# Attention of a hybrid diffusion step: running maxima, biases on ScalarE, weight sums from a column of ones

## The chip, the cores and the metric

The kernel runs on one core of one Trainium2 chip. That core has five engines, each of which runs its own list of instructions in order: TensorE (PE in the profile; its weight loads are shown as PEld), VectorE (DVE), ScalarE (ACT), GpSimd (POOL) and SyncE (SP), which here issues all DMAs. The metric is device time in microseconds (us) of one execution.

## The reference

Two layers are applied to 256 prompt tokens and 2048 latent tokens. Each layer projects the tokens once, runs four mixers beside each other (latent attention, a long convolution called Hyena, a diagonal state space S5, and gated linear attention GLA), gates them and projects back. The change touches the attention alone, which has four heads of query width 96 and value width 64. A latent query reads 512 cached, then 2048 latent keys; a prompt query reads the 256 prompt keys:

```
s  = einsum('bqhd,bkhd->bhqk', q, k) * 96 ** -0.5
pr = softmax(s, axis=-1)
o  = einsum('bhqk,bkhd->bqhd', pr, v)
```

## The kernel before, in words

A unit of attention is one head and one tile of 128 queries. There are 16 latent tiles and 2 prompt tiles, 4 heads and 2 layers, so 128 units with 2560 keys and 16 units with 256. The 2560 keys are cut into three chunks, `CHUNKS = [(0, 1024), (1024, 1024), (2048, 512)]`; a prompt unit has one chunk. Values that must be exact to more than 16 bits are held as a high and a low fp16 part, so a product takes two or three matmuls.

`scores` (line 469) makes one chunk of scores: for each 512 keys three matmuls into one tile `sp` in PSUM (L482 to L484) and a maximum on VectorE (L485); the two maxima of a 1024-key chunk are joined on VectorE (L489) and turned into the bias of the exponential, also on VectorE (L490); ScalarE takes the exponential into `e` and adds up each row into `su` (L492). Each such exponential is followed in the trace by a second ScalarE instruction that reads the sum out (ACTIVATION_READ_ACCUMULATOR). Every chunk has its own maximum.

`values` (line 496) rounds `e` to fp16 on ScalarE or, every third time, on VectorE (L505, L507), takes the remainder on GpSimd (L508), transposes both parts by a DMA (L510, `ph` to `pt`) and multiplies them with the values: per 128 keys one matmul with the high part of the weights against 128 columns (high and low part of `V`), and one with the low part against 64 columns (L514, L515). The three chunks of a unit go to three column blocks of one PSUM tile `om`, of which there is a single buffer.

`combine` (line 517) brings the three chunks to a common maximum: minimum of the biases (L525), factors `al` (L526, ScalarE), the sums times the factors (L527), their total (L528), its reciprocal (L529), the factors times that (L530), and then the three blocks of `om` times their factors, added up (L533, L535), and the high and low columns added (L537). Apart from L526 all of it is on VectorE.

Two chunks are in flight: the loop in `attention` emits the scores of the next chunk before `values` and `combine` of the last one. Heads 0 and 1 come first (stream `side`), heads 2 and 3 later (stream `fill`). Keys and values of a head are loaded by `load` (line 455) into pools of two buffers.

The order of each engine's instructions is not the order of the code: a scheduler plays the whole program through on a model of the machine and, by the priority of each stream, decides which ready instruction of an engine comes next. Hyena, GLA, the filters of the next layer and the output projection run in the same stretches, so what attention takes on an engine also sets where their instructions stand.

Of the kernel before, what the change touches and what calls it, by code (L numbers as in the profile page):

```python
# [8 lines left out]
F32 = mybir.dt.float32  # L9
# [294 lines left out]
def mla_prep(s, l, p, tp, pp):  # L304
# [67 lines left out]
    for t in range(22):  # L372
# [39 lines left out]
        nc.scalar.activation(vd[:, :, 0:64], kv[:, :, 64:128], AF.Copy, scale=sv)  # L412
        nc.vector.scalar_tensor_tensor(out=vd[:, :, 64:128], in0=kv[:, :, 64:128], scalar=sv, in1=vd[:, :, 0:64],
# [38 lines left out]
def attention(s, l, units, tp, kp, bank, ps_o, emit):  # L452
# [17 lines left out]
    def scores(u, c, k0, n):  # L470

        KT = u["KT"]
        e = tp.tile([128, 1024], F32, tag="e", name="e", bufs=3)[:, 0:n]
        nb, su, m = u["nb"], u["su"], u["m"]
        parts = range(0, n, 512)
        sps = []
        for i, a in enumerate(parts):
# [12 lines left out]
        nc.vector.tensor_scalar(out=nb[:, c:c + 1], in0=mc, scalar1=nssc, scalar2=LN2_15, op0=ALU.mult, op1=ALU.add)  # L490
        for i, d in enumerate(sps):
            nc.scalar.activation(e[:, i * 512:min(i * 512 + 512, n)], d, AF.Exp, bias=nb[:, c:c + 1], scale=ssc,  # L492
                                 accum_out=su[:, 2 * c + i:2 * c + i + 1])
        u["e"][c] = e

    def values(u, c, k0, n, first):

        e, V = u["e"].pop(c), u["V"]
        if first:
            u["om"] = ps_o.tile([128, 3, 128], F32, tag="om", name="om")  # L500
# [11 lines left out]
        for i in range(nk):  # L512
            v = V[:, k0 // 128 + i]
            nc.tensor.matmul(om[:, c], lhsT=pt[:, i], rhs=v, start=i == 0, stop=False)  # L514
            nc.tensor.matmul(om[:, c, 0:64], lhsT=pt[:, nk + i], rhs=v[:, 0:64], start=False, stop=i == nk - 1)  # L515

    def combine(u, C):
        nb, su, om = u["nb"], u["su"], u["om"]
        al, dn, mx = small(4, "al"), small(1, "dn"), small(1, "mx")
        w = tp.tile([128, 128], F32, tag="wo", name="wo")  # L520
        sc = su.rearrange("p (c i) -> p c i", i=2)
        last = C - 1
# [31 lines left out]
    for h, t in units:  # L554
        if h not in kv:
            kv[h] = load(h)
        if (h // 2, t) not in pairs:
# [6 lines left out]
        u = dict(h=h, t=t, qt=pairs[h // 2, t][0][:, h % 2], KT=KT, V=V, e={}, m=small(8, "m"), nb=small(4, "nb"), su=small(8, "su"),  # L564
                 ns=5 if t < 16 else 1)
        if C > 1:
            nc.vector.memset(u["su"][:, 5:6], 0.0)
# [1251 lines left out]

PADF = 640  # L1820


def body(tc, I, O, depth=DEPTH):
# [21 lines left out]
    with ExitStack() as top:  # L1845
# [5 lines left out]
        for l in range(depth):  # L1851
# [73 lines left out]
            kp = att.enter_context(pool(name=f"kv{l}", bufs=2, side="right"))  # L1925
            ps_s = att.enter_context(pool(name=f"pss{l}", bufs=3, space=PSUM))
# [89 lines left out]
```

## Time and profile before

| | |
|---|---|
| time, median of 3 runs | 4542.72 us (4534.35 to 4557.65) |
| profiled execution: time, span in the trace | 4533.57 us, 4531.5 us |
| busy in the span: PE, PEld, DVE, ACT, POOL | 3680.5, 2131.0, 3249.0, 2180.7, 2048.0 us |
| the same as shares | 81%, 47%, 72%, 48%, 45% |
| first and last score matmul of attention | 1138.5 us, 4424.4 us |

No engine is busy all the time, and the work of the stages differs: projections fill 0 to about 1133 us and 2455 to 3400 us, attention with its neighbours 1133 to 2455 us (layer 0) and 3400 to 4455 us (layer 1). In the rows further down, `L489` is line 489 of the kernel above, `out<-in` names the tiles of an instruction, and `x256` says how many instructions a row stands for. "Idle before" is the time that the engine waited just before the instructions of a row, and the arrow names what ended the wait.

### The profile page before, as it was taken

To read this page: it belongs to the slowest core of one execution; us is meant where nothing else is said; L and a number is where in the kernel's file an instruction comes from. 1 tells how busy PE (TensorE), PEld (TensorE's weight loads), DVE (VectorE), ACT (ScalarE), POOL (GpSimd) and SP (SyncE) were. 2 spreads that over 40 slices of the span, in tenths; PEclk is the share of its full clock that TensorE was granted. 3 is DMA by queue.
4 is the path that set the end of the run, shared out by engine and by line. 5 is a ranking of instruction groups with operands and counts; after the bars stand their busy time and mean duration, and the time that the engine had idled before them with its cause. 6 is when DMAs were issued, how large, how long until landed. Compare 5 with 4: busy or idle time off the path is not lost.

```text
span 4531.5 us, 67262 instructions
## 1 busy us (share of the span) xinstructions
PE 3680.5 (81%) x21798; PEld 2131.0 (47%) x21798; DVE 3249.0 (72%) x8338; ACT 2180.7 (48%) x4337; POOL 2048.0 (45%) x2052
## 2 busy tenths in 40 slices
PE   6788988778777878778876788889898888667898
PEld 2544544324455555334433644544455555434444
DVE  4765477886788888778774568875447878667884
ACT  3533234546554555675453333363336545646562
POOL 2443343650565655555443234424225545434552
PEclk8999999889888988899998899999998868877999
DMA  6744745656977789896987555633447856999895
GB/s 210 182 120 139 213 122 147 195 136 189 219 184 171 168 203 209 231 243 178 238 204 198 139 132 142 154 105 122 134 147 187 189 135 147 217 233 247 192 187 148
DMA packets 1343432, 799.93 MB, mean 177 GB/s; under 512 B 989588, under 2 KB 1221296, under 8 KB 1341544
## 3 DMA queue, kind: packets, MB, share of 16 engines
q1 hardware_dynamic: 1343080, 795.63, 69.8%
q8 instruction: 173, 2.83, 0.3%
q14 instruction: 179, 1.47, 0.1%
HBM read 352.12 MB, written 207.37 MB: 123 GB/s over the span
## 4 chain that ended last, share of the span: by engine, by line
PE 18%; DVE 16%; DMA 7%; issue 5%; ACT 4%; POOL 2%; SPq 2%; POOLq 0%; DVEq 0%; ACTq 0%
DMA pt<-ph 3%; DVE m L485 2%; PE lv L1603 2%; PE mm L266 2%; PE mm L267 2%; PE mm L268 2%; ACT e L492 2%; DVE m L489 1%; PE mm L1801 1%; PE mm L1802 1%; PE mm L1803 1%; PE sp L482 1%; DVE X L1189 1%; PE om L514 1%; PE sp L484 1%
## 5 line engine op out<-in xcount | busy, mean ns | idle before, releaser
L508 POOL TENSOR_TENSOR ph<-e,ph 128x1024 f16<-128x1024 f32 (+2 forms) x400 | 728.5, 1829 | 636.2 <-ACT ph L505 274.3
L492 ACT ACTIVATE e<-sp,nb,ssc 128x512 f32<-128x512 f32 (+1 forms) x656 | 499.9, 768 | 416.7 <-DVE nb L490 331.6
L266 PE MATMUL mm<-hT,ws 128*128 128x512 f16 (+1 forms) x1440 | 533.0, 370 | 55.1 <-ACT zc L1708 22.5
L485 DVE TENSOR_REDUCE m<-sp 128x1 f32<-128x512 f32 (+1 forms) x656 | 438.6, 676 | 132.6 <-PE sp L484 130.4
L267 PE MATMUL mm<-hT,ws 128*128 128x512 f16 (+1 forms) x1440 | 533.0, 370 | 0.0
L268 PE MATMUL mm<-hT,ws 128*128 128x512 f16 (+1 forms) x1440 | 531.7, 369 | 0.0
L514 PE MATMUL om<-V,pt 128*128 128x128 f16 x2560 | 299.4, 234 | 107.2 <-DMA pt<-ph 60.5
L482 PE MATMUL sp<-KT,qt 128*128 128x512 f16 x640 | 273.0, 427 | 131.3 <-ACT e L492 128.4
L514 PEld LDWEIGHTS <-pt 128*128 128x128 f16 x2592 | 256.2, 108 | 152.7 <-DMA pt<-ph 89.4
L505 ACT CAST ph<-e 128x1024 f16<-128x1024 f32 (+2 forms) x268 | 269.2, 1005 | 88.0 <-DMA pt<-ph 85.8
L515 PE MATMUL om<-V,pt 128*128 128x64 f16 x2560 | 289.7, 205 | 0.0
L515 PEld LDWEIGHTS <-pt 128*128 128x128 f16 x2592 | 245.7, 104 | 62.6 <-issue 48.9
L483 PE MATMUL sp<-KT,qt 128*128 128x512 f16 x640 | 272.6, 426 | 0.0
L484 PE MATMUL sp<-KT,qt 128*128 128x512 f16 x640 | 272.2, 425 | 0.0
L266 PE MATMUL mm<-ws,hT 128*128 128x256 f16 (+1 forms) x864 | 219.1, 268 | 63.8 <-DMA hT<-hl 31.4
L1603 PE MATMUL lv<-qh,kh 32*128 32x128 f32 x1440 | 220.2, 317 | 31.1 <-DVE att L1604 18.3
L267 PEld LDWEIGHTS <-ws 128*128 128x128 f16 x1440 | 145.3, 101 | 213.0 <-issue 90.3
L1801 PE MATMUL mm<-wo,bh 128*128 128x512 f16 x576 | 222.6, 387 | 12.0 <-DVE oy L1804 10.2
L1603 PEld LDWEIGHTS lv<-qh,kh 32*128 32x128 f32 x1440 | 182.4, 212 | 94.7 <-issue 32.7
L1802 PE MATMUL mm<-wo,bh 128*128 128x512 f16 x576 | 222.6, 387 | 4.4 <-DVE wo L1756 4.4
L1803 PE MATMUL mm<-wo,bh 128*128 128x512 f16 x576 | 222.6, 386 | 1.7 <-DVE bh L1776 1.7
L267 PE MATMUL mm<-ws,hT 128*128 128x256 f16 (+1 forms) x864 | 219.9, 268 | 0.0
(520 smaller groups left out, 9426.7 us busy)
## 6 DMA issues: line engine op xcount, KB each, us to landing
kab<-KS SPq DMA_DIRECT2D x128, 256.0 KB
wf<-in_w_in SPq DMA_DIRECT2D x22, 1024.0 KB
b<-br SPq DMA_DIRECT2D x36, 512.0 KB
A1F<-a SPq DMA_DIRECT2D x64, 256.0 KB
zg<-z SPq DMA_DIRECT2D x64, 256.0 KB
b<-A1F SPq DMA_DIRECT2D x32, 512.0 KB
KS<-k SPq DMA_DIRECT2D x64, 256.0 KB
aw<-in_ada_w SPq DMA_DIRECT2D x64, 256.0 KB
```

Of the source, the lines that this page charges most:

```text
L266: nc.tensor.matmul(ps, lhsT=lh, rhs=rh, start=i == 0, stop=False)
L267: nc.tensor.matmul(ps, lhsT=lh, rhs=rl, start=False, stop=False)
L268: nc.tensor.matmul(ps, lhsT=ll, rhs=rh, start=False, stop=i == n - 1)
L482: nc.tensor.matmul(d, lhsT=qh, rhs=kh, start=True, stop=False)
L483: nc.tensor.matmul(d, lhsT=qh, rhs=kl, start=False, stop=False)
L484: nc.tensor.matmul(d, lhsT=ql, rhs=kh, start=False, stop=True)
L485: nc.vector.tensor_reduce(m[:, 2 * c + i:2 * c + i + 1], d, axis=AX.X, op=ALU.max)
L492: nc.scalar.activation(e[:, i * 512:min(i * 512 + 512, n)], d, AF.Exp, bias=nb[:, c:c + 1], scale=ssc, accum_out=su[:, 2 * c + i:2 * c + i ...
L508: nc.gpsimd.tensor_tensor(out=ph[:, n:2 * n], in0=e, in1=ph[:, 0:n], op=ALU.subtract)
L514: nc.tensor.matmul(om[:, c], lhsT=pt[:, i], rhs=v, start=i == 0, stop=False)
L515: nc.tensor.matmul(om[:, c, 0:64], lhsT=pt[:, nk + i], rhs=v[:, 0:64], start=False, stop=i == nk - 1)
L1603: nc.tensor.matmul(ps[:, cc], lhsT=kh[hh, cc], rhs=qh[hh, cc], start=True, stop=True, tile_position=(32 * h, 0))
```

## The change

Four edits are made in the attention, and one in the memory layout.

- Running maxima: the bias of a chunk comes from the maximum over all partial maxima of the unit so far (one VectorE reduction over 2, 4 or 5 columns) instead of this chunk's own. So the last chunk has the unit's maximum and its factor is 1.
- Biases on ScalarE: the bias is computed by an ACTIVATE (Copy with a scale and a constant) instead of a VectorE instruction.
- Sums from a column of ones: the tile of values gets a column of ones, written by GpSimd at each load, so the matmuls of `values` make the sum of the weights as column 128 of `om`. The exponential no longer adds up. For this the low part of the values stands in columns 0 to 63 and the high part in 64 to 127, the matmuls have 129 and 65 columns, and the load writes 128 of the tile's 130 columns.
- `combine`: two factors on ScalarE, the first block scaled on ScalarE, the second multiplied and added on VectorE, the third added on VectorE, then the reciprocal of the sum's column (VectorE), one half scaled (ScalarE), and the other half scaled and added (VectorE).
- A pad of 48 floats a partition is reserved in the pool of keys and values; nothing writes or reads it.

```diff
@@ mla_prep
-        nc.scalar.activation(vd[:, :, 0:64], kv[:, :, 64:128], AF.Copy, scale=sv)
-        nc.vector.scalar_tensor_tensor(out=vd[:, :, 64:128], in0=kv[:, :, 64:128], scalar=sv, in1=vd[:, :, 0:64],
+        nc.scalar.activation(vd[:, :, 64:128], kv[:, :, 64:128], AF.Copy, scale=sv)
+        nc.vector.scalar_tensor_tensor(out=vd[:, :, 0:64], in0=kv[:, :, 64:128], scalar=sv, in1=vd[:, :, 64:128],
@@ load
-            V = kp.tile([128, (b - a) // 128, 128], F16, tag="V" + nm, name="V" + nm)
+            V = kp.tile([128, (b - a) // 128, 130], F16, tag="V" + nm, name="V" + nm)
             nc.sync.dma_start(K, s.KT[l][:, h, :, a:b])
-            nc.sync.dma_start(V, s.V[l][h, :, a // 128:b // 128])
+            nc.gpsimd.memset(V[:, :, 128:129], 1.0)
+            nc.sync.dma_start(V[:, :, 0:128], s.V[l][h, :, a // 128:b // 128])
@@ scores
-        mc = m[:, 2 * c:2 * c + 1]
-        if len(sps) > 1:
-            nc.vector.tensor_tensor(out=mc, in0=mc, in1=m[:, 2 * c + 1:2 * c + 2], op=ALU.max)
-        nc.vector.tensor_scalar(out=nb[:, c:c + 1], in0=mc, scalar1=nssc, scalar2=LN2_15, op0=ALU.mult, op1=ALU.add)
+        mc, k = m[:, 0:1], 2 * c + len(sps)
+        if k > 1:
+            mc = m[:, 5 + c:6 + c]
+            nc.vector.tensor_reduce(mc, m[:, 0:k], axis=AX.X, op=ALU.max)
+        nc.scalar.activation(nb[:, c:c + 1], mc, AF.Copy, scale=nssc, bias=LN2_15)
         for i, d in enumerate(sps):
-            nc.scalar.activation(e[:, i * 512:min(i * 512 + 512, n)], d, AF.Exp, bias=nb[:, c:c + 1], scale=ssc,
-                                 accum_out=su[:, 2 * c + i:2 * c + i + 1])
+            nc.scalar.activation(e[:, i * 512:min(i * 512 + 512, n)], d, AF.Exp, bias=nb[:, c:c + 1], scale=ssc)
@@ values
-            nc.tensor.matmul(om[:, c], lhsT=pt[:, i], rhs=v, start=i == 0, stop=False)
-            nc.tensor.matmul(om[:, c, 0:64], lhsT=pt[:, nk + i], rhs=v[:, 0:64], start=False, stop=i == nk - 1)
+            nc.tensor.matmul(om[:, c], lhsT=pt[:, i], rhs=v[:, 0:129], start=i == 0, stop=False)
+            nc.tensor.matmul(om[:, c, 64:129], lhsT=pt[:, nk + i], rhs=v[:, 64:129], start=False, stop=i == nk - 1)
@@ combine
         if C > 1:
-            nc.vector.tensor_reduce(mx, nb[:, 0:C], axis=AX.X, op=ALU.min)
-            nc.scalar.activation(al[:, 0:C], nb[:, 0:C], AF.Exp, bias=mx, scale=-1.0)
-            nc.vector.tensor_tensor(out=sc[:, 0:C], in0=sc[:, 0:C], in1=al[:, 0:C].unsqueeze(2).to_broadcast([128, C, 2]), op=ALU.mult)
-            nc.vector.tensor_reduce(dn, su[:, 0:u["ns"]], axis=AX.X, op=ALU.add)
-            nc.vector.reciprocal(dn, dn)
-            nc.vector.tensor_scalar(out=al[:, 0:C], in0=al[:, 0:C], scalar1=dn, scalar2=None, op0=ALU.mult)
+            nc.scalar.activation(al, nb[:, 0:2], AF.Exp, bias=nb[:, 2:3], scale=-1.0)
+            nc.scalar.activation(w, om[:, 0], AF.Copy, scale=al[:, 0:1])
+            nc.vector.scalar_tensor_tensor(out=w, in0=om[:, 1], scalar=al[:, 1:2], in1=w, op0=ALU.mult, op1=ALU.add)
+            nc.vector.tensor_tensor(out=w, in0=om[:, 2], in1=w, op=ALU.add)
         else:
-            nc.vector.reciprocal(al[:, 0:1], su[:, 0:1])
-        nc.vector.tensor_scalar(out=w, in0=om[:, last], scalar1=al[:, last:C], scalar2=None, op0=ALU.mult)
-        for c in range(last):
-            nc.vector.scalar_tensor_tensor(out=w, in0=om[:, c], scalar=al[:, c:c + 1], in1=w, op0=ALU.mult, op1=ALU.add)
-        nc.vector.tensor_tensor(out=o[...], in0=w[:, 0:64], in1=w[:, 64:128], op=ALU.add)
+            nc.scalar.copy(w, om[:, 0])
+        nc.vector.reciprocal(dn, w[:, 128:129])
+        nc.scalar.activation(w[:, 0:64], w[:, 0:64], AF.Copy, scale=dn)
+        nc.vector.scalar_tensor_tensor(out=o[...], in0=w[:, 64:128], scalar=dn, in1=w[:, 0:64], op0=ALU.mult, op1=ALU.add)
@@ body
+            kp.tile([128, PADK], F32, name="pad", bufs=1)
```

The scheduler places the new instructions. On VectorE, near the end of layer 1, this stood in its order before, over about one unit (`m` are the maxima, `wo` the combined block, `oy` a row of the output projection):

```order
L485 TENSOR_REDUCE m<-sp 128x1 x2
L535 SCALAR_TENSOR_TENSOR wo<-om,al,wo 128x128
L485 TENSOR_REDUCE m<-sp 128x1
L489 TENSOR_TENSOR m<-m 128x1
L535 SCALAR_TENSOR_TENSOR wo<-om,al,wo 128x128
L490 TENSOR_SCALAR nb<-m,nssc_30528 128x1 x2
L537 TENSOR_TENSOR o<-wo 128x64
L525 TENSOR_REDUCE mx<-nb 128x1
L507 CAST ph<-e 128x512
```

In the changed kernel the same place on VectorE reads so, where L486, L491, L526, L527, L530 and L533 are the maxima, the running maximum, the two block sums, the reciprocal and the last step:

```order
L486 TENSOR_REDUCE m<-sp 128x1 x2
L527 TENSOR_TENSOR wo<-om,wo 128x129
L486 TENSOR_REDUCE m<-sp 128x1
L491 TENSOR_REDUCE m<-m 128x1
L530 RECIPROCAL nb<-wo 128x1
L491 TENSOR_REDUCE m<-m 128x1
L533 SCALAR_TENSOR_TENSOR o<-wo,nb 128x64
L508 CAST ph<-e 128x512
L486 TENSOR_REDUCE m<-sp 128x1
```

The biases and the sums are gone from VectorE, and each tensor-with-tensor maximum has become a reduction. On ScalarE, in the same stretch, there stood before:

```order
L492 ACTIVATE e,su<-sp,nb,ssc_30526 128x512 x2
L526 ACTIVATE al<-nb,mx 128x3
L492 ACTIVATE e,su<-sp,nb,ssc_30526 128x512 x3
L1775 ACTIVATE bh<-b,bps 128x1024
L505 CAST ph<-e 128x1024 x2
L492 ACTIVATE e,su<-sp,nb,ssc_30526 128x512 x2
```

In the changed kernel ScalarE's order has the biases (L492), the factors (L524) and the two scalings of `combine` (L525, L531) between the exponentials (L494):

```order
L525 ACTIVATE wo<-om,nb 128x129
L1765 ACTIVATE bh,bss<-b 128x1024
L506 CAST ph<-e 128x1024
L492 ACTIVATE nb<-m,nssc_30065 128x1
L531 ACTIVATE wo<-wo,nb 128x64
L506 CAST ph<-e 128x1024
L494 ACTIVATE e<-sp,nb,ssc_30063 128x512 x2
L492 ACTIVATE nb<-m,nssc_30065 128x1 x2
L524 ACTIVATE nb<-nb 128x2
L494 ACTIVATE e<-sp,nb,ssc_30063 128x512 x3
```

So L525, which needs the unit's last matmul, and L531, which needs VectorE's reciprocal, stand in front of the next exponentials on ScalarE. GpSimd's order in layer 1 has the write of the ones (L464) among the remainders (L509) and Hyena's products (L884), where before there was nothing between them:

```order
L509 TENSOR_TENSOR ph<-e,ph 128x1024
L464 MEMSET V 128x20
L509 TENSOR_TENSOR ph<-e,ph 128x1024
L884 TENSOR_TENSOR xs<-xs,kab 128x512
L509 TENSOR_TENSOR ph<-e,ph 128x512
```

The write needs the last matmul of the head that had the buffer before, and stands in GpSimd's queue with everything behind it.

## Rows read from the trace of the kernel before

**Rows 1.** two stretches: us; busy PE, PEld, DVE, ACT, POOL; clock; DMA share; GB/s
```profile
1133.00:2455.00 1322.00, 1050.38 (x6715) 624.56 (x6713) 1053.13 (x2467) 730.58 (x1417) 707.62 (x531) 0.88 0.85 204
3400.00:4455.00 1055.00, 836.67 (x5644) 521.99 (x5643) 815.89 (x1930) 579.97 (x1167) 545.93 (x392) 0.85 0.84 193
```

**Rows 2.** chain that ended last, by line, share of the stretch 3400 to 4455
```profile
by line: DMA pt<-ph 9.2%; DVE m L485 8.3%; issue 6.0%; PE lv L1603 5.6%; DVE m L489 5.1%; ACT e L492 4.7%; PE sp L482 3.1%; PE om L514 2.9%; PE h L933 2.8%; PE sp L484 2.7%; PE sp L483 2.7%; DMA kab<-KS 2.6%; POOL ph L508 2.2%; SPq L510 2.1
```

**Rows 3.** view of the waits, whole span: who waited for whom, us, times, longest
```profile
ACT e L492 <- DVE nb L490: 331.6, 131, 8.8
DVE m L485 <- PE sp L484: 130.4, 125, 5.6
PE sp L482 <- ACT e L492: 130.3, 77, 6.1
```

**Rows 4.** timeline at 4245: start us, us, engine, line, operation, idle before
```profile
4245.82 2.13 POOL L508 TENSOR_TENSOR ph<-e,ph 128x1024 f16<-128x1024 f32 x1 [3.44 <-ACT ph L505]
4245.92 2.06 DVE L527 TENSOR_TENSOR su<-su,al 128x6 f32<-128x6 f32 x1 [1.19 <-ACT al L526]
```

**Rows 5.** lines L489 and L528: durations ns min/median/max, first and last start
```profile
L489 DVE TENSOR_TENSOR m<-m x256: 139/160/2273, 1143.7 to 4421.1; 128x1 f32<-128x1 f32 x128
L528 DVE TENSOR_REDUCE dn<-su x128: 120/148/160, 1155.5 to 4425.8; 128x1 f32<-128x5 f32 x128
```

**Rows 6.** groups of VectorE: count, busy us, mean ns, idle before and its releasers
```profile
L489 DVE TENSOR_TENSOR m<-m 128x1 f32<-128x1 f32 x256 | 156.3, 610 | 1.0
L535 DVE SCALAR_TENSOR_TENSOR wo<-om,al,wo 128x128 f32<-128x128 f32 x256 | 88.1, 344 | 2.8
L530 DVE TENSOR_SCALAR al<-al,dn 128x3 f32<-128x3 f32 x128 | 75.2, 588 | 1.4
L490 DVE TENSOR_SCALAR nb<-m,nssc 128x1 f32<-128x1 f32 x400 | 74.6, 204 | 1.8
L537 DVE TENSOR_TENSOR o<-wo 128x64 f32<-128x64 f32 x144 | 70.1, 487 | 1.3
L527 DVE TENSOR_TENSOR su<-su,al 128x6 f32<-128x6 f32 x128 | 64.4, 503 | 26.1 <-ACT al L526 14.8 <-ACT e L492 11.0
L533 DVE TENSOR_SCALAR wo<-om,al 128x128 f32<-128x128 f32 x144 | 49.6, 344 | 50.5 <-PE om L515 50.1
L525 DVE TENSOR_REDUCE mx<-nb 128x1 f32<-128x3 f32 x128 | 19.1, 149 | 1.9
L528 DVE TENSOR_REDUCE dn<-su 128x1 f32<-128x5 f32 x128 | 19.1, 149 | 1.2
```

**Rows 7.** chain, 3400 to 4455: first and last piece of the removed lines
```profile
3412.83 1.56 DVE m L489
...
4422.35 0.04 DVE mx L525
```

**Rows 8.** groups of ScalarE
```profile
L492 ACT ACTIVATION_READ_ACCUMULATOR e<-sp,nb,ssc 128x1 f32 x656 | 129.2, 197 | 0.0
L526 ACT ACTIVATE al<-nb,mx 128x3 f32<-128x3 f32 x128 | 37.9, 296 | 24.3 <-DVE mx L525 24.0
L402 ACT COPY ct<-mm 128x256 f32<-128x256 f32 x36 | 13.1, 365 | 19.6 <-PE mm L401 19.3
```

**Rows 9.** groups of TensorE
```profile
L514 PE MATMUL om<-V,pt 128*128 128x128 f16 x2560 | 299.4, 234 | 107.2 <-DMA pt<-ph 60.5 <-DVE gt L1940 18.9 <-DVE wo L535 16.9
L515 PE MATMUL om<-V,pt 128*128 128x64 f16 x2560 | 289.7, 205 | 0.0
```

**Rows 10.** windows of 100 us: first and last of the full-DMA slices
```profile
1100.00:1200.00 100.00, 66.76 (x472) 36.25 (x470) 64.24 (x161) 66.99 (x124) 39.41 (x38) 0.82 0.98 284
...
4100.00:4200.00 100.00, 67.59 (x423) 39.97 (x424) 77.87 (x182) 62.52 (x116) 49.31 (x27) 0.74 0.96 241
```

**Rows 11.** chain: a store of 128 KB of values, a load of 640 KB
```profile
2653.48 2.41 DMA V<-vd
...
4011.45 7.60 DMA V<-V
```

More of the change, by code (lines that the diff above doesn't have):

```diff
@@ L473, in scores @@
         e = tp.tile([128, 1024], F32, tag="e", name="e", bufs=3)[:, 0:n]
-        nb, su, m = u["nb"], u["su"], u["m"]
-        parts = range(0, n, 512)
+        nb, m = u["nb"], u["m"]
         sps = []
-        for i, a in enumerate(parts):
+        for i, a in enumerate(range(0, n, 512)):
             w = min(512, n - a)
@@ L499, in values @@
         if first:
-            u["om"] = ps_o.tile([128, 3, 128], F32, tag="om", name="om")
+            u["om"] = ps_o.tile([128, 3, 129], F32, tag="om", name="om")
         om = u["om"]
@@ L513, in values @@
             v = V[:, k0 // 128 + i]
-            nc.tensor.matmul(om[:, c], lhsT=pt[:, i], rhs=v, start=i == 0, stop=False)
-            nc.tensor.matmul(om[:, c, 0:64], lhsT=pt[:, nk + i], rhs=v[:, 0:64], start=False, stop=i == nk - 1)
+            nc.tensor.matmul(om[:, c], lhsT=pt[:, i], rhs=v[:, 0:129], start=i == 0, stop=False)
+            nc.tensor.matmul(om[:, c, 64:129], lhsT=pt[:, nk + i], rhs=v[:, 64:129], start=False, stop=i == nk - 1)
     def combine(u, C):
-        nb, su, om = u["nb"], u["su"], u["om"]
@@ L519, in combine @@
[L519 to L522, printed above, removed]
-        if C > 1:
-            nc.vector.tensor_reduce(mx, nb[:, 0:C], axis=AX.X, op=ALU.min)
-            nc.scalar.activation(al[:, 0:C], nb[:, 0:C], AF.Exp, bias=mx, scale=-1.0)
-            nc.vector.tensor_tensor(out=sc[:, 0:C], in0=sc[:, 0:C], in1=al[:, 0:C].unsqueeze(2).to_broadcast([128, C, 2]), op=ALU.mult)
-            nc.vector.tensor_reduce(dn, su[:, 0:u["ns"]], axis=AX.X, op=ALU.add)
-            nc.vector.reciprocal(dn, dn)
-            nc.vector.tensor_scalar(out=al[:, 0:C], in0=al[:, 0:C], scalar1=dn, scalar2=None, op0=ALU.mult)
-        else:
-            nc.vector.reciprocal(al[:, 0:1], su[:, 0:1])
@@ L533, in combine @@
-        nc.vector.tensor_scalar(out=w, in0=om[:, last], scalar1=al[:, last:C], scalar2=None, op0=ALU.mult)
-        for c in range(last):
-            nc.vector.scalar_tensor_tensor(out=w, in0=om[:, c], scalar=al[:, c:c + 1], in1=w, op0=ALU.mult, op1=ALU.add)
+        nb, om = u["nb"], u["om"]
+        al, dn = nb[:, 3:5], nb[:, 5:6]
+        w = tp.tile([128, 129], F32, tag="wo", name="wo")
+        if C > 1:
+            nc.scalar.activation(al, nb[:, 0:2], AF.Exp, bias=nb[:, 2:3], scale=-1.0)
+            nc.scalar.activation(w, om[:, 0], AF.Copy, scale=al[:, 0:1])
+            nc.vector.scalar_tensor_tensor(out=w, in0=om[:, 1], scalar=al[:, 1:2], in1=w, op0=ALU.mult, op1=ALU.add)
+            nc.vector.tensor_tensor(out=w, in0=om[:, 2], in1=w, op=ALU.add)
+        else:
+            nc.scalar.copy(w, om[:, 0])
@@ L536, in combine @@
+        nc.vector.reciprocal(dn, w[:, 128:129])
+        nc.scalar.activation(w[:, 0:64], w[:, 0:64], AF.Copy, scale=dn)
         o = pairs[u["h"] // 2, u["t"]][1]
-        nc.vector.tensor_tensor(out=o[:, u["h"] % 2 * 64:u["h"] % 2 * 64 + 64], in0=w[:, 0:64], in1=w[:, 64:128], op=ALU.add)
+        nc.vector.scalar_tensor_tensor(out=o[:, u["h"] % 2 * 64:u["h"] % 2 * 64 + 64], in0=w[:, 64:128], scalar=dn, in1=w[:, 0:64],
+                                       op0=ALU.mult, op1=ALU.add)
     turn = [0]
@@ L563, in attention @@
         KT, V = kv[h][t >= 16]
[L564 to L567, printed above, removed]
+        u = dict(h=h, t=t, qt=pairs[h // 2, t][0][:, h % 2], KT=KT, V=V, e={}, m=small(8, "m"), nb=small(8, "nb"))
         for c, (k0, n) in enumerate(chunks):
@@ L1817, in outproj @@
             nc.sync.dma_start((O["y_sample"][0] if lat else O["y_prompt"][0])[o:o + 128], y)
+PADK = 48
 PADF = 640
```

## The prediction

> **What bounds the kernel now.** I read the page for the shares, then the windows of the two attention stretches, the chain that ended last, the waits, and the groups by line. No engine is full on average, but the two attention stretches together take 2377 of 4531 us, and in them VectorE is busy 1053 and 816 us, 80% and 77%; TensorE's record is as busy, the 16 DMA engines 85% and 84%, ScalarE and GpSimd some 55% [rows 1]. The chain through the second stretch changes hands all the time: DMA transposes 9.2%, the score maxima on VectorE 8.3%, the joining of two maxima (L489) 5.1%, the exponentials 4.7%, GLA's and Hyena's matmuls [rows 2]. The waits show the same as a loop: ScalarE waits for the bias from VectorE (331.6 us, 131 times), VectorE for the score matmuls (130.4), these for the exponential that frees their bank (130.3) [rows 3]. The longest of them ends in VectorE's L490, so attention runs at the pace at which VectorE gets from a finished score to a bias.
>
> VectorE is slow there for a reason that the timeline shows. At 4245.92 an instruction over 6 columns lasts 2.06 us and ends with the GpSimd remainder that began 0.10 us before it and lasts 2.13 us [rows 4]. Over all, L489, on a single column, has a median of 160 ns, a maximum of 2273 and a mean of 610; the reduction L528 never takes over 160 ns [rows 5]. So instructions of VectorE with two tensors in SBUF stand still while GpSimd makes a remainder, and small reductions and instructions with one operand in PSUM (L535, mean 344) do not.
>
> **The change part by part.** *VectorE.* Removed: L489 156.3, L490 74.6, L525 19.1, L527 64.4, L528 19.1, L530 75.2, L533 49.6, L535 88.1 and L537 70.1 us, together 616.5 [rows 6]. The 144 reciprocals stay as many; a memset that goes is small. Added: three reductions for each of 128 units, 384 x 149 ns = 57.2 (the price of L525 and L528); a scaled sum and a plain sum per unit, each with one operand in PSUM like L535, 256 x 344 = 88.1; the last step, 144 times, with both tensors in SBUF as L537 has them, so I leave it its 487 ns with the standstill, 70.1. Together 215.4; VectorE is relieved of 401 us. A reduction could cost as much as L489 at worst, 610 ns; I take 149, since two lines of that very form show it.
>
> *ScalarE.* The sum's read-out goes from all 656 exponentials, 129.2 us. Added are 400 biases, 128 + 16 copies of 129 columns out of PSUM and 144 scalings of 64 columns. The nearest rows are L526, 3 columns with a bias read from a tile, 296 ns, and L402, 256 columns from PSUM, 365 ns; the read-out itself, 197 ns, is the smallest. With 296 for biases and scalings and 330 for the copies: 118.4 + 42.6 + 47.5 = 208.5, so ScalarE gets 79 us more; with 197 for all 688 it would be 6, with 365, 122 [rows 8]. At 55% busy it has room; on the loop, a bias costs 0.30 us on ScalarE where it cost 0.20 on VectorE, and two exponentials cost 0.39 less.
>
> *TensorE.* One column more in 5184 matmuls. L514 and L515 differ by 64 columns and 29 ns, 0.45 ns a column, 2.4 us in all [rows 9]. The swapped halves of the values in `mla_prep` and the pad issue nothing new.
>
> *Loads of V.* Eight loads of 640 KB now land in pieces of 128 columns, 256 bytes. One old load stands in the chain with 7.60 us; a store of 128 KB in 256-byte pieces with 2.41, which scales to 12.0 for five times as much [rows 11]. So a load costs 0 to 4.4 us more, 8 x 4.4 = 35 at worst. In each layer two of the four loads are issued before attention starts, so I count half: 18 us. The page "DMA: Bandwidth & Descriptors" of the Trainium skill, section "Why small descriptors are slow", counts 11 cycles for 256 bytes where 8 would do; by that estimate a load costs 7.60 x 11/8 = 10.5 us and the half comes to 11 us. The two rows point the same way and somewhat further. The write of the ones waits for the last matmul of the head two before; behind it in GpSimd's queue stand the remainders. It happens eight times a run with 20 columns and I cost it at nothing; if TensorE is late there, it costs some us each.
>
> *What of it lies on the path.* In the second stretch the chain holds 341 pieces of the removed or moved lines, 132.0 us: L489 72 pieces and 54.4 us, L490 78 and 14.1, L527 26 and 16.4, L530 21 and 8.2, L533 and L535 74 and 21.0, L537 23 and 13.6, L525 and L528 47 and 4.3 [rows 7]. Put back: reductions for L489, 72 x 1.5 x 0.149 = 16.1; biases on ScalarE, 78 x 0.296 = 23.1; the block sums 21.0 and the last step 13.6 unchanged; 73.8. The exponential's 4.7% of 1055 us is 49.6 [rows 2], of which the read-out, 197 of its 965 ns, is 10.1. So the path loses 132.0 - 73.8 + 10.1 = 68 us. The chain through most of the first stretch isn't shown; it has as many units and a busier VectorE, so I take the same: 137 for both. Five of some 24 slices of 100 us in the stretches have the DMA engines at 0.95 or more, from 1100 to 4100 us [rows 10]; there I count no gain: 137 x 19/24 = 108 us. As an upper bound stands VectorE's whole relief, 401; as a lower one nothing.
>
> Sum, against the profiled execution: 4533.6 - 108 + 18 = **4444 us**. That execution lies 9 us below the median of the runs shown, 4542.7; I leave the forecast at 4444.
>
> **The rivals.** *A, VectorE is the bound all along.* For it: 80% and 77% busy, and an in-order queue in which a standstill of 2 us delays GLA and Hyena too, so that more than the chain's pieces goes. Against: the chain is on VectorE for some lines only, transposes lead it. Half of the relief of 401 us: 4333 us.
>
> *B, the transposes set the pace.* For it: they head the chain with 9.2%, and the DMA share is 0.84 and more. If attention can't go faster than its transposes, only what lies outside them is gained, about a quarter of 108, and the loads take 18 of it back: 4533.6 - 27 + 18 = 4525.
>
> *C, ScalarE's queue becomes the wait.* The first block's copy waits for the unit's last matmul, and the scaling of one half for VectorE's reciprocal; both stand in ScalarE's list ahead of the next biases and exponentials, and the single `om` is freed only by a sum that comes after the copy. 128 + 144 such waits, each like today's wait for a bias, 331.6 / 131 = 2.53 us: 688 us of standing if all occur. From 36 of them on the path (36 x 2.53 = 90) the gain is gone; with 60 the time is 4444 + 152 = 4596. Against: the queue order puts other work between, and L526, which waits for VectorE in the same way today, cost ScalarE 24 us over 128 units [rows 8].
>
> *D, the change doesn't do what it says.* If the running maximum stood still behind GpSimd like L489, 610 ns, the 72 x 1.5 pieces would cost 65.9 and not 16.1, the path would lose 18.5 us per stretch, and 4533.6 - 29 + 18 = 4522 remains. Row L528 speaks against it.
>
> The scheduler also lays out Hyena, GLA and the output projection anew; that can help or hurt by some tens of us in any of these cases and widens them all.
>
> **How the numbers follow.** Forecast 0.63 (its own range 4375 to 4510), A 0.13, B 0.10, C 0.11, D 0.03. A change of 0.5% is about what a measurement of this kernel can tell from none, so faster means below 4520, slower above 4565. Faster: the forecast and A, 0.76; the same: B and D, 0.13; slower: C, 0.11. The range that holds 8 in 10 reaches into A below and up to B and the near side of C: 4330 to 4545.
>
> **What would show it.** In the new profile, VectorE should be busy about 2850 us; the running maximum should have a mean near 150 ns and no maximum of 2 us, the last step still one; no read-outs after the exponentials; ScalarE near 2260 us. In the waits, the 331.6 us on the bias should be nearly halved. The chain through the second stretch should hold less VectorE and more transposes. I am wrong if ScalarE's waits for the reciprocal and the last matmul add up to over 100 us (C), if the DMA share goes to 0.95 with little gained (B), or if both stretches shrink by over 90 us each (A).

## The result and the profile after

The changed kernel takes 4456.30 us in the median of 4 runs (4444.55 to 4475.89), the kernel before 4538.53 in 4 runs beside it: a ratio of 0.984 [0.9808, 0.9872], 1.6% less. The profiled execution took 4445.36 us (span 4443.5 us) where the forecast had 4444; by the medians the gain is 82 us where 90 were forecast. That the sum came out so close is partly luck, as the stages show.

| | before | after |
|---|---|---|
| busy in the span: PE, DVE, ACT, POOL, us | 3680.5, 3249.0, 2180.7, 2048.0 | 3627.2, 2983.1, 2290.1, 2065.5 |
| scores of layer 0 over the latent keys, first to last matmul, us | 1249 | 1176 |
| from there to the end of layer 0's output projection, us | 98 | 112 |
| input projection of layer 1, us | 891 | 918 |
| scores of layer 1 over the latent keys, us | 1014 | 958 |
| from there to the end, us | 114 | 104 |

The two attention stages gave 73 and 56 us, 129 together; 27 went back in the projection of layer 1, 15 behind the scores of layer 0 and 9 ahead of attention and in the gaps between the stages, and 10 more came from the end: 88 us of span in all. The windows that answer to [rows 1] (same columns) show VectorE 114 us less busy in each, ScalarE 72 and 46 more, and the DMA share up. They are the same times and not quite the same work: the second runs past the end of the changed kernel at 4443.5 us.

```profile
1133.00:2455.00 1322.00, 1061.73 (x6848) 635.73 (x6847) 938.77 (x1992) 802.66 (x1453) 728.09 (x544) 0.89 0.89 213
3400.00:4455.00 1055.00, 837.35 (x5810) 510.92 (x5809) 701.19 (x1405) 625.54 (x1163) 552.36 (x393) 0.90 0.86 198
```

TensorE's granted clock in the second window is 0.90, where it was 0.85; both are means over its two levels, 1.2 and 2.4 GHz. In the whole span TensorE is 53 us less busy, although the matmuls of `values` have one column more. So a part of the gain may be TensorE running at the higher level for longer; it was not separated from the shorter waits.

VectorE's new lines, for [rows 6] (count, busy us, mean ns, idle before and its releaser), with the casts (L508), which the change doesn't touch, and below them the same casts before:

```profile
L533 DVE SCALAR_TENSOR_TENSOR o<-wo,nb 128x64 f32<-128x64 f32 x144 | 111.9, 777 | 42.0 <-ACT wo L531 41.7
L508 DVE CAST ph<-e 128x512 f16<-128x512 f32 x120 | 106.2, 885 | 70.0 <-DMA pt<-ph 48.1 <-ACT e L494 19.2 <-POOL oy L1799 2.1
L526 DVE SCALAR_TENSOR_TENSOR wo<-om,nb,wo 128x129 f32<-128x129 f32 x128 | 44.3, 346 | 43.5 <-ACT wo L525 43.1
L527 DVE TENSOR_TENSOR wo<-om,wo 128x129 f32<-128x129 f32 x128 | 36.5, 285 | 1.2
L491 DVE TENSOR_REDUCE m<-m 128x1 f32<-128x2 f32 (+2 forms) x384 | 54.8, 146 | 1.8
```

```profile
L507 DVE CAST ph<-e 128x512 f16<-128x512 f32 x120 | 83.9, 699 | 54.3 <-ACT e L492 30.6 <-DMA pt<-ph 20.9 <-POOL hv L1023 1.6
```

The same lines' spread, for [rows 5] (shortest, median, longest ns; first and last start):

```profile
L491 DVE TENSOR_REDUCE m<-m x384: 92/145/170, 1149.8 to 4343.6; 128x1 f32<-128x2 f32 x64, 128x1 f32<-128x5 f32 x64, 128x1 f32<-128x4 f32 x64
...
L533 DVE SCALAR_TENSOR_TENSOR o<-wo,nb x144: 263/296/2725, 1187.0 to 4394.0; 128x64 f32<-128x64 f32 x144
```

The running maximum never stands still; the last step does. The timeline near 4203 us shows both beside GpSimd's remainder (start, us, engine, line, operation, idle before; rows between them left out), as [rows 4] did for before:

```profile
4203.67 2.13 POOL L509 TENSOR_TENSOR ph<-e,ph 128x1024 f16<-128x1024 f32 x1 [2.86 <-ACT ph L506]
...
4203.82 2.06 DVE L533 SCALAR_TENSOR_TENSOR o<-wo,nb 128x64 f32<-128x64 f32 x1
...
4206.11 2.12 POOL L509 TENSOR_TENSOR ph<-e,ph 128x1024 f16<-128x1024 f32 x1 [0.31 <-DMA pt<-ph]
4206.52 0.16 DVE L491 TENSOR_REDUCE m<-m 128x1 f32<-128x4 f32 x1
```

L533 begins 0.15 us after a remainder and ends 0.08 us after it; L491 begins 0.41 us after the next one and is through in 0.16 us. The Trainium skill, page "SBUF — State Buffer", section "Who interferes with whom", says the same of Trainium2: a reduction never contends with GpSimd, an instruction with two inputs in SBUF does against one that reads SBUF, and whoever comes later waits. The rows agree, 170 against 2725 ns at the longest.

ScalarE's new lines, for [rows 8], and the waits, for [rows 3]:

```profile
L492 ACT ACTIVATE nb<-m,nssc 128x1 f32<-128x1 f32 x400 | 113.7, 292 | 286.4 <-DVE m L491 278.0 <-DVE o L533 5.8 <-DVE m L486 1.5
L531 ACT ACTIVATE wo<-wo,nb 128x64 f32<-128x64 f32 x144 | 49.5, 344 | 36.4 <-DVE nb L530 35.8
L525 ACT ACTIVATE wo<-om,nb 128x129 f32<-128x129 f32 x128 | 47.0, 367 | 58.0 <-PE om L516 57.1
L524 ACT ACTIVATE nb<-nb 128x2 f32<-128x2 f32 x128 | 37.6, 294 | 0.4
```

```profile
ACT nb L492 <- DVE m L491: 278.0, 155, 6.9
DVE m L486 <- PE sp L485: 186.8, 153, 7.7
...
PE sp L483 <- ACT e L494: 103.4, 70, 8.1
...
ACT wo L529 <- PE om L516: 15.2, 6, 3.4
```

ScalarE's wait for VectorE fell from 331.6 to 278.0 us. It now occurs 155 times and not 131, but lasts 1.79 us in the mean where it lasted 2.53. VectorE waits longer for scores (186.8 against 130.4), and the score matmuls less for the exponentials (103.4 against 130.3), so the loop's longest hand-over is no longer so far above the others. The chain that ended last says what took it over. The chain of after can be followed back no farther than 3932 us. Over the last 496 us of before and the last 494 of after, its shares by line begin so, first before, then after:

```profile
by line: DMA pt<-ph 13.8%; DVE m L485 8.8%; issue 7.3%; DVE m L489 6.0%; PE mm L1801 5.8%; ACT e L492 5.8%; PE mm L1803 5.7%; PE mm L1802 5.7%; POOL ph L508 3.1%; DMA wof<-in_w_out 2.4%; DVE ph L507 2.2%; DVE oy L1804 2.1%; SPq L510 1.9%; A
```

```profile
by line: DMA pt<-ph 25.1%; issue 8.6%; POOL ph L509 7.1%; SPq L511 6.2%; DVE m L486 4.3%; PE mm L1795 4.1%; PE mm L1796 4.0%; PE mm L1797 4.0%; ACT ph L506 3.7%; ACT e L494 3.2%; DVE ph L508 3.2%; POOL oy L1799 2.8%; DVE o L533 1.9%; PE sp 
```

The joined maximum (6.0%) is gone from the front, its successor L491 holds 2.1 of 494 us, the score maxima fell by half, and the transposes with the remainders before them and the queue that issues them took their place: 18.8% before, 38.4% after.

### The profile page after: what moved, and what is told of

The parts are those of the page before. It is cut to its first block, busy times and chain, and to the rows that moved or that the text cites. A ratio compares the mean times of both kernels' runs of the same rounds, so it can differ in the third digit from the quotient of the medians.

```text
span 4443.5 us, 66247 instructions
## 1 busy us (share of the span) xinstructions
PE 3627.2 (82%) x21798; PEld 2100.2 (47%) x21798; DVE 2983.1 (67%) x7282; ACT 2290.1 (52%) x4369; POOL 2065.5 (46%) x2068
## 5 line engine op out<-in xcount | busy, mean ns | idle before, releaser
L509 POOL TENSOR_TENSOR ph<-e,ph 128x1024 f16<-128x1024 f32 (+2 forms) x400 | 723.6, 1813 | 542.2 <-ACT ph L506 286.3
L486 DVE TENSOR_REDUCE m<-sp 128x1 f32<-128x512 f32 (+1 forms) x656 | 436.9, 676 | 188.0 <-PE sp L485 186.8
L494 ACT ACTIVATE e<-sp,nb,ssc 128x512 f32<-128x512 f32 (+1 forms) x656 | 473.8, 768 | 21.4 <-POOL ph L509 10.5
L515 PE MATMUL om<-V,pt 128*128 128x129 f16 x2560 | 303.5, 233 | 111.7 <-DMA pt<-ph 77.3
L483 PE MATMUL sp<-KT,qt 128*128 128x512 f16 x640 | 263.6, 412 | 103.6 <-ACT e L494 102.4
L516 PE MATMUL om<-V,pt 128*128 128x65 f16 x2560 | 293.4, 203 | 0.0
L484 PE MATMUL sp<-KT,qt 128*128 128x512 f16 x640 | 263.1, 411 | 0.0
L492 ACT ACTIVATE nb<-m,nssc 128x1 f32<-128x1 f32 x400 | 113.7, 292 | 286.4 <-DVE m L491 278.0
L485 PE MATMUL sp<-KT,qt 128*128 128x512 f16 x640 | 261.1, 408 | 0.0
L267 PEld LDWEIGHTS <-ws 128*128 128x128 f16 x1440 | 144.7, 100 | 211.8 <-issue 90.3
L268 PEld LDWEIGHTS <-ws 128*128 128x128 f16 x1440 | 145.0, 101 | 157.7 <-issue 35.3
```

Of the source, the lines that this page charges most:

```text
L267: nc.tensor.matmul(ps, lhsT=lh, rhs=rl, start=False, stop=False)
L268: nc.tensor.matmul(ps, lhsT=ll, rhs=rh, start=False, stop=i == n - 1)
L509: nc.gpsimd.tensor_tensor(out=ph[:, n:2 * n], in0=e, in1=ph[:, 0:n], op=ALU.subtract)
L515: nc.tensor.matmul(om[:, c], lhsT=pt[:, i], rhs=v[:, 0:129], start=i == 0, stop=False)
L516: nc.tensor.matmul(om[:, c, 64:129], lhsT=pt[:, nk + i], rhs=v[:, 64:129], start=False, stop=i == nk - 1)
```

## The experiments

Two theories on the gain stand against each other in the expectations. Theory 1, the standstill: the time comes from VectorE's instructions with two tensors in SBUF, which stand still behind GpSimd ahead of a bias; their number on that path decides. Theory 2, the order: any edit makes the scheduler lay the program out anew, and that moves the time. The table also bears on a third: any work taken from VectorE, or the read-outs taken from ScalarE, counts alike. Several forecasts missed: e3 moved by 9.0% where theory 1 had at most 0.5%, e1 gained less than its 0.985, e4 and e6 came out faster than either theory had them, e7 and e11 lay in the order's range and outside theory 1's, and e8 fell between its two ranges. All ratios are against the kernel before, run on the same chip. The stages of all runs, from their score matmuls over the latent keys and their projection matmuls, in us:

| kernel | ratio | scores 0 | projection 1 | scores 1 | DVE busy |
|---|---|---|---|---|---|
| before | 1 | 1249 | 891 | 1014 | 3249 |
| changed | 0.984 [0.9808, 0.9872] | 1176 | 918 | 958 | 2983 |
| e1 joined maximum a reduction | 0.9912 [0.988, 0.9945] | 1217 | 917 | 994 | 3132 |
| e2 biases on ScalarE | 1.0005 [0.9982, 1.0028] | 1209 | 914 | 973 | 3157 |
| e12 maxima and biases, old combine | 0.9953 [0.9935, 0.9971] | 1214 | 905 | 967 | 3132 |
| e5 changed, maxima of two tensors | 1.0065 [1.003, 1.01] | 1251 | 892 | 1035 | 3102 |
| e6 changed, with read-outs | 0.9747 [0.9718, 0.9776] | 1172 | 889 | 980 | 3001 |
| e7 changed, last step a reduction | 0.976 [0.9734, 0.9785] | 1182 | 888 | 946 | 2914 |
| e8 like e7, all casts on ScalarE | 0.9848 [0.9821, 0.9874] | 1186 | 912 | 969 | 2840 |
| e4 changed, no pad | 0.9752 [0.9719, 0.9786] | 1160 | 897 | 948 | 2984 |
| e11 like e7, no pad | 0.9813 [0.9788, 0.9838] | 1160 | 891 | 955 | 2924 |
| e13 changed, pad 24 | 0.9822 [0.9789, 0.9856] | 1178 | 917 | 952 | 2994 |
| e9 before, pad 24 | 1.0006 [0.9987, 1.0025] | 1251 | 891 | 998 | 3233 |
| e3 before, pad 48 | 1.0902 [1.0868, 1.0935] | 1000 | 889 | 1239 | 3247 |

**e1, one part alone: the joined maximum.** Only the instruction of L489 is another.

```diff
-            nc.vector.tensor_tensor(out=mc, in0=mc, in1=m[:, 2 * c + 1:2 * c + 2], op=ALU.max)
+            mc = m[:, 5 + c:6 + c]
+            nc.vector.tensor_reduce(mc, m[:, 2 * c:2 * c + 2], axis=AX.X, op=ALU.max)
```

> The kernel before with one edit: the two maxima of a 1024-key chunk are joined by a reduction over two columns, not by a maximum of two tensors. Theory 1 (VectorE's standstill behind GpSimd on attention's loop): the 256 joins fall from a mean of 610 ns to about 147, VectorE is relieved of about 118 us, and of the chain's 54.4 us in the second stretch 72 x 0.147 = 10.6 remain, so 44 us go per stretch, times 19/24: 69 us, a ratio of 0.985. Theory 2 (the gain comes from the order that the scheduler lays out anew for any change): the ratio is as far from 1 as that of the kernel with the pad alone, in either direction, and doesn't follow VectorE's relief.

It took 4483.27 us against 4520.69. The group of the joined maximum, 156.3 us before [rows 6], fell to this:

```profile
L490 DVE TENSOR_REDUCE m<-m 128x1 f32<-128x2 f32 x256 | 36.6, 143 | 1.0
```

The standstill of 120 us is gone, and 37 us of time with it, about half of the gain. Taken alone that is no more than another order can move (e4, below), so e1 points at the standstill but doesn't prove it; e5 does more.

**e2, one part alone: the biases on ScalarE.**

```diff
-        nc.vector.tensor_scalar(out=nb[:, c:c + 1], in0=mc, scalar1=nssc, scalar2=LN2_15, op0=ALU.mult, op1=ALU.add)
+        nc.scalar.activation(nb[:, c:c + 1], mc, AF.Copy, scale=nssc, bias=LN2_15)
```

> The kernel before with one edit: the 400 biases are made on ScalarE. Theory 1: VectorE loses 75 us of work, ScalarE gets 117 us (292 ns each); on the path a bias of 0.29 us takes the place of one of 0.20, some +9 us per stretch, while VectorE's queue is shorter: ratio 0.997 to 1.005. Theory 2: any ratio within the spread of the pad-only kernel.

No difference, though VectorE is 92 us less busy. The waits (engine, line, releaser, us, times, longest) show that ScalarE now waits for the maxima themselves, 411 us against 331.6:

```profile
ACT nb L490 <- DVE m L489: 314.7, 145, 7.3
...
ACT nb L490 <- DVE m L485: 96.7, 58, 7.4
```

Both score stages are some 40 us shorter, and the projection (+23 us), the stretches behind the scores (+17 and +28) and the gaps give it back. Most likely other streams' work was only moved behind the scores; that was not shown. A stage by itself is not the time.

**e5, one part undone: the maxima by instructions of two tensors**, in the changed kernel.

```diff
-            nc.vector.tensor_reduce(mc, m[:, 0:k], axis=AX.X, op=ALU.max)
+            if len(sps) > 1:
+                nc.vector.tensor_tensor(out=mc, in0=m[:, 2 * c:2 * c + 1], in1=m[:, 2 * c + 1:2 * c + 2], op=ALU.max)
+            else:
+                nc.vector.tensor_tensor(out=mc, in0=m[:, 2 * c:2 * c + 1], in1=m[:, 4 + c:5 + c], op=ALU.max)
+            if c and len(sps) > 1:
+                nc.vector.tensor_tensor(out=mc, in0=mc, in1=m[:, 4 + c:5 + c], op=ALU.max)
```

> The changed kernel with the running maximum made by maxima of two tensors (four per unit of three chunks) instead of three reductions. Theory 1 (standstill of VectorE's two-tensor instructions on attention's loop): 512 of them at about 600 ns take 310 us of VectorE where 56 were taken, and on the path twice the 54.4 us per stretch that the kernel before had in its chain, 93 us more per stretch, times 19/24: some 147 us, a ratio of 1.01 against the kernel before. Theory 2 (the order laid out anew makes the difference): 0.975 to 0.99 like the other forms of the changed kernel.

It took 4557.82 us against 4525.62: the whole gain is gone and 0.65% more. Its three lines of maxima stand still, and ScalarE waits for them for 404.9 us:

```profile
L492 DVE TENSOR_TENSOR m<-m 128x1 f32<-128x1 f32 x256 | 150.6, 588 | 1.0
L496 DVE TENSOR_TENSOR m<-m 128x1 f32<-128x1 f32 x128 | 70.3, 549 | 1.4
L494 DVE TENSOR_TENSOR m<-m 128x1 f32<-128x1 f32 x128 | 41.9, 328 | 2.4
```

```profile
ACT nb L497 <- DVE m L496: 224.8, 91, 7.7
ACT nb L497 <- DVE m L492: 160.2, 74, 6.6
...
ACT nb L497 <- DVE m L494: 19.9, 17, 3.8
```

That is twice as many such instructions as before had, so it is more than an undoing. Against the changed kernel it is 2.3% slower, over twice what order was seen to move (e4), and outside the 0.975 to 0.99 of theory 2, while theory 1 had 1.01. VectorE's busy time, 3102 us, is still 147 below before's and the kernel is slower: what counts is the standstill ahead of a bias, not how much VectorE does. Theory 1 holds, and the third theory falls. An estimate of what the maxima are worth, by proportion: they took 156.3 us of VectorE before, 54.8 in the changed kernel and 262.8 here, so of the 2.3% about half, 1.1%, lies between before and changed. With e1's 0.9% that is the larger part of the 1.6%.

**e12, the maxima and biases with the old combine.** `scores` as changed, except that the exponentials still add up; all else as before.

```diff
-            nc.vector.tensor_tensor(out=mc, in0=mc, in1=m[:, 2 * c + 1:2 * c + 2], op=ALU.max)
-        nc.vector.tensor_scalar(out=nb[:, c:c + 1], in0=mc, scalar1=nssc, scalar2=LN2_15, op0=ALU.mult, op1=ALU.add)
+            mc = m[:, 5 + c:6 + c]
+            nc.vector.tensor_reduce(mc, m[:, 0:k], axis=AX.X, op=ALU.max)
+        nc.scalar.activation(nb[:, c:c + 1], mc, AF.Copy, scale=nssc, bias=LN2_15)
```

> The kernel before with the running maxima and the biases on ScalarE, but the old combine, the old sums and no column of ones. The standstill theory: 384 reductions for 256 joins (-100 us of VectorE) and the biases (-75) are in, the two-tensor and small instructions of combine (about 225 us) not: ratio 0.988 to 0.995, so that combine and the sums are worth some 1%. If the maxima alone made the gain: 0.974 to 0.985.

It gains 0.5%, at the edge of the 0.988 to 0.995 of theory 1, and less than e1, which does less; 0.4% between the two is within what order moves. The rest of the change's 1.6% may come from the new combine and the sums, which take L525, L527, L528, L530 (two of them with means of 503 and 588 ns in [rows 6]) off VectorE. That is not shown: it is a difference of two kernels, hardly over what order moves, and the old maxima with the new combine were not run.

**e6, one part undone: the read-outs.** The exponentials add up again into a tile that nothing uses; the pad is 16, so that the rest lies where it lay.

```diff
-            nc.scalar.activation(e[...], d, AF.Exp, bias=nb[:, c:c + 1], scale=ssc)
+            nc.scalar.activation(e[...], d, AF.Exp, bias=nb[:, c:c + 1], scale=ssc,
+                                 accum_out=u["su"][:, 2 * c + i:2 * c + i + 1])
...
-        u = dict(..., nb=small(8, "nb"))
+        u = dict(..., nb=small(8, "nb"), su=small(8, "su"))
...
-PADK = 48
+PADK = 16
```

> The changed kernel with the exponentials still summing their rows into a tile that nothing reads (the pad is cut to 16 floats so that all addresses stay). Theory 1: 656 read-outs of 197 ns come back, ScalarE is busy 129 us more, about 10 us per stretch on the path: ratio 0.987 to 0.990. Rival (ScalarE has become the bound of the loop): the whole 129 us comes back, ratio 1.01.

```profile
L494 ACT ACTIVATION_READ_ACCUMULATOR e<-sp,nb,ssc 128x1 f32 x656 | 128.5, 196 | 0.0
```

The 128.5 us are back on ScalarE, which is busy 2345.4 us and so only 55 more than in the changed kernel (busy time counts overlapping instructions once), and the kernel is no slower than that one (0.9747). No price of the read-outs can be seen; the 10.1 us a stretch that the sum gave them are below what the order alone moves (e4, below).

**e7, the last step as a reduction** over the two halves, scaled afterwards on ScalarE.

```diff
-        nc.scalar.activation(w[:, 0:64], w[:, 0:64], AF.Copy, scale=dn)
-        nc.vector.scalar_tensor_tensor(out=o[...], in0=w[:, 64:128], scalar=dn, in1=w[:, 0:64], op0=ALU.mult, op1=ALU.add)
+        nc.vector.tensor_reduce(o, w[:, 0:128].rearrange("p (a d) -> p d a", a=2), axis=AX.X, op=ALU.add)
+        nc.scalar.activation(o, o, AF.Copy, scale=dn)
```

> The changed kernel with the last step of combine turned round: VectorE adds the two halves by a reduction over a strided view (one tensor as input), ScalarE then scales the 64 sums; as many instructions as before. Theory 1: the 144 last steps, a mean of 777 ns with standstill, become about 300 ns, VectorE is relieved of some 68 us, the path of 8 to 20 us: ratio 0.978 to 0.983. Theory 2: within the spread of order, 0.972 to 0.990, with VectorE's relief not telling which.

```profile
L532 DVE TENSOR_REDUCE o<-wo 128x64 f32<-128x128 f32 x144 | 38.7, 269 | 0.0
```

The step costs 38.7 us of VectorE and not 111.9. With the pad of 48 the ratio is 0.976 where the changed kernel has 0.984; so far it looked like a gain.

**e8, relief of VectorE where nothing waits for it.** On top of e7 every cast is on ScalarE (`if turn[0] % 3:` becomes `if True:`).

> The kernel with the turned last step, and all fp16 roundings of the weights on ScalarE (before, every third is on VectorE). Theory 1: VectorE is relieved of a further 115 us (132 roundings, mean 870 ns with standstill), ScalarE gets 84 us more (613 ns each); as ScalarE is at 52%, the ratio falls to 0.970 to 0.980. Rival (ScalarE's list is the loop by now): ratio above 0.985.

VectorE falls by 73 us more, to 2840.3, and nothing is gained: the ratio is 0.9848 where e7 has 0.976, a difference no larger than what order moves. VectorE now waits for ScalarE's block copy, 119.5 us where e7 has 53.2, and for scores, 275.3 where e7 has 171.7:

```profile
DVE m L486 <- PE sp L485: 275.3, 189, 7.1
ACT nb L492 <- DVE m L491: 204.8, 128, 6.5
DVE wo L526 <- ACT wo L525: 119.5, 46, 8.5
```

**e4, e11 and e13: the same work in other places, and two of them in another order.** The changed kernel and e7 without the pad (the line of `body` goes), and the changed kernel with `PADK = 24`.

> The changed kernel without the pad. Theory 1: the attention stretches are as short as in the changed kernel (1187 and 966 us from first to last score matmul) within 15 us each, the ratio is 0.980 to 0.989. Theory 2: the ratio goes back to above 0.99.

> The version with the turned last step, without the pad: the candidate for the fastest. The standstill theory expects 0.970 to 0.977, as the turned step and the missing pad each gave 0.975 to 0.976; the order theory anything from 0.972 to 0.986.

> The changed kernel with a pad of 24 floats instead of 48, no overlap of GLA's and Hyena's tiles: the same work in another order. With the pad of 48 the ratio was 0.984, without pad 0.975. If these two differ by their order alone, this one lies between 0.972 and 0.987; a value outside would say that the spread of order is wider still.

The pad issues nothing, yet without it the changed kernel has 0.9752 and not 0.984, and e7 without it 0.9813 and not 0.976: it goes both ways. The traces show what differs. Without the pad (e4) another matmul than in the changed kernel stands at 12380 of the 21798 places in TensorE's order. With 24 floats (e13) all instructions of TensorE, VectorE, ScalarE and GpSimd stand in the order of the changed kernel, at other addresses, and the time is the same, 0.9822 against 0.984. So e13 is no sample of another order, as its expectation took it to be; it shows that this shift of the addresses doesn't move the time. Up to 0.9% between two kernels of this program is the order that the scheduler came to; why the missing pad changes it was not looked into. Over the changed kernel, e4, e7 and e11, the last step as a reduction gives 0.9786 in the mean, the step as changed 0.9796: no effect that can be told, although it takes 70 us from VectorE. Nor can e6's 0.975 be put down to the read-outs.

**e3 and e9, the pad alone** in the kernel before, 48 and then 24 floats.

```diff
             kp = att.enter_context(pool(name=f"kv{l}", bufs=2, side="right"))
+            kp.tile([128, 48], F32, name="pad", bufs=1)
```

> The kernel before with nothing but the pad of 48 floats in the pool of keys and values: the same instructions, other addresses, and so another order from the scheduler. Theory 1: the ratio stays within 0.995 to 1.005. Theory 2: it moves by more than 0.5%, and if it is near 0.984 the pad made the gain.

> The kernel before with a pad of 24 floats, half of the pad alone run before. In the built programs GLA's highest tile (its gate, written from the left) ends at byte 85888 of a partition; Hyena's lowest tile (yt, from the right) begins at 85984 in the kernel before, at 85792 with the pad of 48 floats, and at 85888 with this one. Theory A (the 9% of the pad come from that overlap of 96 bytes, through which GLA's gate had to wait for Hyena): no overlap here, ratio 0.99 to 1.01. Theory B (any shift of the addresses costs as much): ratio 1.05 or more. If A holds, this is also a second sample of the order for the same work as before.

48 floats cost 9.0%, 24 nothing; with 24 TensorE, ScalarE and GpSimd have the order of before, so e9 is no second sample of the order either. In the built programs GLA's highest tile ends at byte 85888 of a partition, and Hyena's lowest begins at 85984 before, at 85888 with 24 floats, and at 85792, 96 bytes inside GLA's tile, with 48. Then GLA must wait until Hyena is through, whose last matmul of layer 0 ends at 1768 us in e3. The row of GLA's matmul L1603 (count, durations, first and last start) of before and of e3 shows it start 656 us later and end 747 us later:

```profile
L1603 PE MATMUL lv<-qh,kh x1440: 269/270/578, 1204.9 to 3820.2; 32*128 32x128 f32 x180
```

```profile
L1603 PE MATMUL lv<-qh,kh x1440: 269/416/578, 1860.7 to 4567.1; 32*128 32x128 f32 x180
```

In the changed kernel the attention's other tiles are smaller by 192 bytes a partition, and its pad of 192 bytes puts Hyena back where it was, so the pad is harmless there, and by e4 not needed.

## Why the prediction was right, and where its terms were not

- **The bound and the mechanism** were right: the loop through VectorE's joined maximum set attention's pace, it stood still behind GpSimd, and a reduction doesn't (e1, e5). The running maximum has 146 ns where 149 were forecast, so rival D falls. Only the class of instructions was drawn too narrowly: L530, which reads one tensor and one factor a partition, stood still too, and so did the casts, with one tensor (2350 ns at the longest before): all 18 of the casts that took over 1.5 us, and 10 of 12 of L530's, ended within 0.3 us of a GpSimd instruction that had begun ahead of them. The spread of L530 before (shortest, median, longest ns):

```profile
L530 DVE TENSOR_SCALAR al<-al,dn x128: 210/228/2349, 1157.2 to 4428.6; 128x3 f32<-128x3 f32 x128
```

- **The path term, 108 us.** The score stages are 129 us shorter, 73 and 56 where 54 each were forecast. Its parts are less sure: the biases alone gave nothing (e2), and of the read-outs nothing can be seen (e6).
- **VectorE's relief was mis-sized**: 401 us forecast, 266 measured. The step that failed is "I leave it its 487 ns with the standstill": L533 has 777 and costs 111.9 us, not 70.1, and the untouched casts grew from 83.9 to 106.2, together 64 us. Why they stood still longer was not settled. In e5, with the standing maxima back, the same two lines have means of 623 and 699 ns, as if the standstill moved to what is left; but in e1, with the joins alone gone, the casts did not grow (656). The other half of the gap is only counting: the groups of the view add up to 3676 us before and 3344 after, 332 less, while busy time counts overlapping instructions once.
- **ScalarE** got 109 us more, not 79. The prices held: biases 292 ns for 296, copies 367 for 330, scalings 344 for 296, together 214.5 us with the 16 copies of the prompt units where 208.5 were forecast. Less the read-outs' 129.2 that makes 85 us, near the 79. Busy time rose by more since it counts overlapping instructions once, and the read-outs had overlapped most: e6 shows 128.5 us of them to add 55. The Trainium skill, page "ScalarE: Activation LUTs", section "What ACT_TABLE_LOAD costs", gives about 280 ns plus 0.833 ns an element for an ACTIVATE with one operand that holds a value for each partition, as the bias instruction's scale does; by that estimate it costs 281 ns, and the row has 292.
- **"Nearly halved"** was wrong: the wait for VectorE fell from 331.6 to 278.0 us, 16%. A bias still comes only behind the score maxima, 640 of them at 683 ns each, and e2's waits show the same: take one cause away and ScalarE waits for the next.
- **The V loads, 18 us, were not there.** In all one wait of 1.2 us lies behind them:

```profile
L465 SPq DMA_DIRECT2D V<-V x8: 371/443/1193, 1117.9 to 3933.2; - x8
...
  POOL ph L509: 1.2, 1
```

- **The projection of layer 1, +27 us, was in no term.** TensorE is 5 us busier in it (776 against 771) and waits 146 us against 124. Here are its largest waits in that stage, then three windows around the longest of them (columns as in [rows 1]):

```profile
PE mm L266 <- ACT z L1679: 23.4, 6, 14.5
PE mm L398 <- DVE cn L388: 18.6, 7, 7.2
PE mm L266 <- ACT zs L1718: 16.4, 2, 8.8
```

```profile
2788.00:2796.00 8.00, 7.69 (x36) 3.23 (x33) 7.30 (x21) 2.00 (x5) 3.38 (x5) 1.00 0.58 143
2796.00:2804.00 8.00, 1.78 (x6) 1.06 (x7) 7.96 (x28) 0.00 (x0) 3.07 (x3) 0.82 0.51 128
2804.00:2812.00 8.00, 8.00 (x25) 3.13 (x23) 6.73 (x22) 3.61 (x11) 3.90 (x8) 0.76 0.49 122
```

TensorE stands around 2800 us while VectorE is busy throughout (7.96 of 8 us) and ScalarE idle, and the granted clock, 1.00 in the first window, is 0.76 in the last. But that wait is not the 27 us: the three lines that make `z` (L1649, L1670 and L1679 here) hold TensorE up for 25.7 us in the changed kernel and for 29.3 before, only in other pieces. The waits for L1718 and L388 grew, by 11 and 8 us, and several smaller ones did. The stage takes 905 to 918 us in six kernels (changed, e13, e1, e2, e8, e12) and 888 to 897 in the other eight; what makes an order slow there stays open.
- **Rival C.** My mark for it was passed: ScalarE's waits for the last matmul and the reciprocal are 57.1 + 15.2 + 35.8 = 108 us, over the 100 I named, and the kernel was not slower. The mark left out that ScalarE had 48% of its time free and that its wait for the bias would fall by 54 us. In e8, with yet more in ScalarE's list, VectorE does wait longer for ScalarE, but its loss against e7 is within what order moves. **A** wanted over 90 us from both stages and B a DMA share of 0.95 with little gained; there were 73 and 56, and 0.91 and 0.90 inside the score stages.

So 4444 was hit because terms that were not there cancelled: 129 where 108 stood, nothing where 18 stood, and +27, +15, +9 and -10 that no term had. The order alone moves this program by up to 0.9%, some 40 us, so a forecast of one sum can't be better than that. Versions faster than both kernels came out on the way (e4, e6 and e7, 4407.69 to 4419.48 us, 0.975 to 0.976); by e11 that is a find among orders rather than an edit to carry on.

## What to carry to other kernels

Where VectorE's tiny instructions have a median of 150 ns and a mean of 600, look for GpSimd beside them, and turn those that others wait for into reductions; the ones nobody waits for may stay. Work taken off an engine buys no time by itself: 92 us of biases, 129 us of read-outs and 70 us of last steps gave nothing here that could be seen. Before an edit of a scheduled program is credited with less than 1%, run the same work in another order, and compare the orders in the traces: a pad of 24 floats left it as it was.

## What the runs showed that was not expected

- 96 bytes of overlap between two pools cost 9.0% [8.68, 9.35] (e3), and nothing in the code shows it: only GLA's first matmul at 1860.7 us and not at 1204.9 does.
- Lines that were left stood still longer: the last step's mean went from 487 (L537) to 777 ns (L533), the casts' from 699 to 885, with GpSimd's remainders unchanged in number (400).
- Taking out a pad that nothing touches makes the changed kernel 0.9% faster (e4) and e7 0.5% slower (e11), by another order; halving it changes neither order nor time (e13).
